# Latent tiles as raw-weight buffers from step 5 of the plain products, and product 6's loads and additions one and two steps later

## Chip, cores and metric

The kernel runs on 1 core of one Trainium2 chip. The metric is device microseconds of one execution; the time of a kernel is the median of its runs.

## What is computed

One decoder layer on 512 tokens of width 2048 in fp32, cut to what matters here:

```
h    = RMSNorm(x) * (1 + scale) + shift
proj = h @ W_in                       # 2048 x 13632
q_lat, kv_lat, k_rope, z_mla, u, v, z_sgu, g_mla, g_sgu = split(proj)
A = causal latent attention(q_lat, kv_lat, k_rope) * silu(z_mla)
B = u * (tril(W_s) v_chunk + b_s) * silu(z_sgu)
x = RMSNorm(x + gate * ((sigmoid(g_mla) * A + sigmoid(g_sgu) * B) @ W_out))
```

Every weight is used once, so the weights stream from HBM; every fp32 matmul is made of three matmuls of rounded parts (high x high, high x low, low x high).

## The kernel before

**Weights.** A `Stream` object `ws` brings each granule of weights through four stages in order. `dma_to` issues its transfer on SyncE's queue into a raw buffer; `cast_to` lets ScalarE write the high part (L139); `split_to` lets VectorE write the low part, raw minus high (L151); `get` hands both to TensorE. A raw buffer comes free when the low part is written. `look` says how many granules beyond the last split one are wanted, and no more are loaded than there are raw buffers (`held == len(self.raws)`). A buffer is either a 1024-wide tile (transfer at L98) or a pair of 512-wide tiles with a transfer for each half (L105). At first there are three: wraw0, wraw1, wraw2.

**The stretch in question.** The latents come first (16 granules of `w1`, 16 of `w2`); their last five blocks stay in PSUM banks `ps2[0..4]` and are copied to `lat8` to `lat12` (L566) by functions in `pend`, two at the first following step and one at each after. Then follow 64 steps, written out in `steps`, one granule each. The number of a granule is its step plus 32; it is the second number in the name of a tile (`wraw2_41` is step 9).

- Steps 0 to 7 ("v"): plain products into four banks and one bank z (L185 to L187).
- Steps 8 to 63: the seven products of a Strassen scheme on two sets of columns, "a" (512 wide) and "b" (384 wide), all matmuls at L701: a1 in steps 8 to 11, b1 in 12 to 15, a5 in 16 to 19, a6 in 20 to 23, b5 in 24 to 27, a2 in 28 to 31, and so on.
- Products 6, 2 and 4 need sums of weight quarters. For set a, a quarter is loaded into a chain tile raw4 to raw7 (`chain_load`, L294, SyncE's queue), and the next quarters are added to it by accumulating transfers on POOL's queue (`chain_add`, L284), which wait for the chain load to land. These granules take no raw buffer.

The normalised latents `lat0` to `lat7` lie in SBUF until they are scaled (`lat_scale`, at steps 0, 1, 1 and 3 for lat4 to lat7) and stored to DRAM (`stores`, L604, in the step after). From step 8 on, `more_raws` adds three raw buffers: w2l and the pairs (lat4, lat5) and (lat6, lat7).

**What sets the order.** The program is written in the order in which each engine runs it: step t first calls `get_step` (split of t+1, from step 10 on also the cast of t+2, transfers ahead), then the matmuls, then the small work listed by `at_step` (evacuations, squares, sums of x for the Strassen operands: `make_sums`, `split_41`), then stores. ScalarE, VectorE and SyncE each take their instructions in that order, so one that waits holds up all behind it on its engine.

After step 63 the remaining column pairs follow by the same scheme in slots of eight triples of matmuls (L1498 to L1500); their first raw weights go into wraw0 and wraw2 (`load`, L862).

Of the kernel before, what the change touches and what calls it, by code (L numbers as in the profile page):

```python
# [165 lines left out]
def trunk_layer(ctx, tc, xT, xn, c, vecs, pos, wada, w1, w2, wv, wv3, wv4, wh, wh15, wq, wqr, wk, wvv, wo, wsT, bsp, gfin, out,  # L166
# [39 lines left out]
    def nt(p, shape, dt, tag, **kw):  # L206
        uid[0] += 1
        return p.tile(shape, dt, tag=tag, name=f"{tag}_{uid[0]}", **kw)
# [10 lines left out]
    latp = Scope("lat", side=RIGHT)  # L219
    ws = Stream(nc, [(wp, f"wraw{i}") for i in range(3)], [(wp, f"w{i}") for i in range(2)])  # L220
# [58 lines left out]
    c1 = [None]  # L279
# [12 lines left out]
    def chain_load(i, c, n):  # L292
        chain[i] = t = nt(c1[0].p, [P, GW], F32, f"raw{4 + i}")
        DMA.dma_start(t[:, :n], wpair[c][0, i])  # L294
        return [t[:, :n]]

    def chain_add(i, src, n):
        return both([chain[i][:, :n]], src)
# [210 lines left out]
    def dot_to(n):  # L509
        nonlocal n_dot  # L510
        while n_dot < min(n, KC):
            ada_dot(n_dot)
            n_dot += 1
# [3 lines left out]
    def fix_to(n, between=None):  # L517

        nonlocal n_fix
        for f in rows_left:  # L520
            f()
        rows_left.clear()
        if n_fix >= min(n, KC):
            if between:
                between()
            return
        js = range(n_fix, min(n, KC))
        assert n_dot >= js[-1] + 1
        n_fix = js[-1] + 1
        cols = slice(js[0], n_fix)  # L530
        tt(shift[:, cols], dots[:, cols], vec[:, C_BADA + js[0]:C_BADA + n_fix], ALU.add)
        ts_ = []
        for j in js:
            t = nt(xq.p, [P, S], F32, "t", bufs=2)
            stt(t, xt[j], gxA[:, j:j + 1], rx, ALU.mult, ALU.mult)
            ts_.append(t)
        for j, t in zip(js, ts_):
            hh[j], hl[j] = parts_tiles(j)
            ACT.activation(hh[j], t, AF.Identity, bias=shift[:, j:j + 1])
        if between:  # L540
            between()
        for j, t in zip(js, ts_):
            stt(hl[j], t, shift[:, j:j + 1], hh[j].bitcast(F32), ALU.add, ALU.subtract)
            rows_left.append(lambda t=t, j=j: ACT.activation(xt[j], t, AF.Identity, bias=shift[:, j:j + 1]))
# [11 lines left out]
    for j in range(KC):  # L556
# [5 lines left out]
            DVE.reciprocal(out=rx[:, j * P:(j + 1) * P], in_=rx[:, j * P:(j + 1) * P])  # L562
        dot_to(DOTS[j])
        fix_to(FIXED[j])
    for m in (3, 0, 1, 2, 4):
        pend.append(lambda m=m: ACT.copy(lat[8 + m], ps2[m]))  # L566


# [33 lines left out]
    def stores():  # L602
        for dst, src in leaving:
            DMA.dma_start(dst, src)  # L604
        leaving[:], made[:] = made[:], []
# [130 lines left out]
    def run_step(t_, wH, wL):  # L736
        c, p, i = steps[t_]
        if c == "v":
            w = VW[c]
            if i == 0:  # L740
                open_banks(c, w)
                open_banks("z", S)
            for k in range(2):
                j = 2 * i + k
                sl = slice(k * w, (k + 1) * w)
                for n in range(NB):
                    tk = slice(n * P, (n + 1) * P)
                    mm3(psv[c][n], hh[j][:, tk], hl[j][:, tk], wH[:, sl], wL[:, sl], j == 0, j == KC - 1)
                sl = slice(2 * w + k * P, 2 * w + (k + 1) * P)
                mm3(psv["z"][0], wH[:, sl], wL[:, sl], hh[j], hl[j], j == 0, j == KC - 1)  # L750
        else:
            block(c, p, i, wH, wL)
        for f in early.pop(t_, ()):
            f()
# [3 lines left out]
    def get_step(t_, **kw):  # L758
        if t_ < 10:
            return get(gv[t_], **kw)  # L760
        return get(gv[t_], ahead=int(t_ < n_steps - 1), cast=gv[min(t_ + 2, n_steps - 1)], **kw)

    for t_ in range(n_steps - 4):
        if t_ == 10:
            ws.his, ws.next_hi = [(c1[0].p, "w2h", 48, 0), ws.his[1], ws.his[0]], 0
        wH, wL = get_step(t_, run=2 if t_ == 0 else 1)
        if t_ < 8:
            fix_to(FIXED[KC + t_], lambda: dot_to(DOTS[KC + t_]))
        if t_ == 8:
            ada.close()  # L770
            c1[0] = Scope("c1", side=RIGHT)
            for j in range(8):
                nt(c1[0].p, [P, S], F32R, f"e{j}")
            nt(c1[0].p, [P, GW + 48], F32R, "w2h")
            ws.more_raws([(c1[0].p, "w2l"), (latp.p, ("lat4", "lat5")), (latp.p, ("lat6", "lat7"))])
            ws.look = 9
            for i in range(4):
                chain_load(i, "a", GW)
        if t_ == 9:
            for i in range(4):  # L780
                chain_add(i, wv[1, i], GW)
        run_step(t_, wH, wL)
        stores()
# [1164 lines left out]
```

## Time and profile before

| quantity | value |
|---|---|
| median of 3 runs | 1551.08 us (1550.26 to 1553.08) |
| the profiled execution's own time | 1548.87 us |
| its span, first to last instruction | 1547.2 us |
| mean granted TensorE clock | 0.997 |
| TensorE busy | 1529.8 us (99%) |
| VectorE busy | 1194.1 us (77%) |
| ScalarE busy | 785.2 us (51%) |
| DMA engines, SyncE's queue / POOL's queue | 51.1% / 20.8% of 16 engines' span |
| HBM read / written | 310.24 / 23.94 MB |

A page of the profile describes one execution. Busy shares are averages over stages; what a change in one stage is worth is read from the timeline and the waits of that stage. A row of the timeline gives start, duration, engine, line, operation, written tile <- read tiles, form, and in brackets the idle time before it and the engine that ended it. Buffer numbers are left out of names, so `wraw` is any of wraw0 to wraw2. A DMA's own row on a queue is its issue; "us to landing" is a separate figure.

### The profile page before, as it was taken

To read this page: it belongs to the slowest core of one execution; us is meant where nothing else is said; L and a number is where in the kernel's file an instruction comes from. 1 tells how busy PE (TensorE), PEld (TensorE's weight loads), DVE (VectorE), ACT (ScalarE), POOL (GpSimd) and SP (SyncE) were. 2 spreads that over 40 slices of the span, in tenths; PEclk is the share of its full clock that TensorE was granted. 3 is DMA by queue.
4 is the path that set the end of the run, shared out by engine and by line. 5 is a ranking of instruction groups with operands and counts; after the bars stand their busy time and mean duration, and the time that the engine had idled before them with its cause. 6 is when DMAs were issued, how large, how long until landed. Compare 5 with 4: busy or idle time off the path is not lost.

```text
span 1547.2 us, 27348 instructions
## 1 busy us (share of the span) xinstructions
PE 1529.8 (99%) x10632; PEld 1425.6 (92%) x10632; DVE 1194.1 (77%) x1856; ACT 785.2 (51%) x1379; POOL 111.2 (7%) x136
## 2 busy tenths in 40 slices
PE   9999989999999999999999999999999999999997
PEld 8888978899999999999999999999888888888886
DVE  8989868878787888877787777777788888854543
ACT  4444456565645455454555646556555555632322
POOL 0000001011011111111111111121000000000000
PEclk9999999999999999999999999999999999999999
DMA  9978489788999998998888888887544344245423
GB/s 378 385 274 313 168 269 266 232 210 226 280 267 272 261 248 252 267 259 210 220 233 251 223 242 244 221 201 217 165 142 133 126 132 139 84 166 182 138 81 109
DMA packets 134580, 335.97 MB, mean 217 GB/s; under 512 B 15385, under 2 KB 39985, under 8 KB 129713
## 3 DMA queue, kind: packets, MB, share of 16 engines
q1 hardware_dynamic: 116146, 275.76, 51.1%
q0 software_dynamic: 18160, 58.20, 20.8%
q8 instruction: 83, 1.36, 0.3%
q14 instruction: 47, 0.39, 0.1%
q10 hardware_dynamic: 144, 0.26, 0.0%
HBM read 310.24 MB, written 23.94 MB: 216 GB/s over the span
## 4 chain that ended last, share of the span: by engine, by line
PE 96%; DVE 1%; DMA 1%; ACT 1%; issue 0%; DVEq 0%; POOL 0%; ACTq 0%; POOLq 0%
PE ps L1499 16%; PE ps L1498 16%; PE ps L1500 16%; PE ps L185 12%; PE ps L186 12%; PE ps L187 12%; PE ps L701 8%; PE ps L1677 1%; DMA wraw<-in_wv 1%; PE ps L1058 1%; PE ps L1641 1%; PE ps L1640 1%; PE ps L501 0%; DVE w0l L151 0%; DVE wada L176 0%
## 5 line engine op out<-in xcount | busy, mean ns | idle before, releaser
L1498 PE MATMUL ps<-h,w2h 128*128 128x256 f32 x408 | 113.8, 279 | 0.0
L1498 PE MATMUL ps<-h,w0h 128*128 128x256 f32 x408 | 113.0, 277 | 0.0
L1500 PE MATMUL ps<-h,w2l 128*128 128x256 f32 x408 | 112.7, 276 | 0.0
L1500 PE MATMUL ps<-h,w0l 128*128 128x256 f32 x408 | 112.7, 276 | 0.0
L1499 PE MATMUL ps<-h,w2h 128*128 128x256 f32 x408 | 112.7, 276 | 0.0
L1499 PE MATMUL ps<-h,w0h 128*128 128x256 f32 x408 | 112.7, 276 | 0.0
L1498 PE MATMUL ps<-h,w1h 128*128 128x256 f32 x400 | 110.9, 277 | 0.0
L1500 PE MATMUL ps<-h,w1l 128*128 128x256 f32 x400 | 110.5, 276 | 0.0
L1499 PE MATMUL ps<-h,w1h 128*128 128x256 f32 x400 | 110.5, 276 | 0.0
L139 ACT CAST w0h<-wraw 128x1024 fp32r<-128x1024 f32 (+5 forms) x71 | 61.1, 870 | 76.3 <-issue 25.3
L151 DVE TENSOR_TENSOR w0l<-wraw,w0h 128x1024 fp32r<-128x1024 f32 (+5 forms) x69 | 68.3, 997 | 39.1 <-ACT w0h L139 38.1
L173 DVE TENSOR_TENSOR w0l<-raw,w0h 128x1024 fp32r<-128x1024 f32 x56 | 68.5, 1223 | 30.0 <-ACT w0h L884 29.2
L139 ACT CAST w1h<-wraw 128x1024 fp32r<-128x1024 f32 (+5 forms) x67 | 53.9, 811 | 72.2 <-PE ps L187 24.9
L185 PE MATMUL ps<-h,w1h 128*128 128x512 f32 x218 | 86.6, 397 | 0.0
L151 DVE TENSOR_TENSOR w1l<-wraw,w1h 128x1024 fp32r<-128x1024 f32 (+5 forms) x61 | 57.8, 951 | 36.9 <-ACT w1h L139 35.7
L186 PE MATMUL ps<-h,w1h 128*128 128x512 f32 x218 | 85.0, 390 | 0.0
L187 PE MATMUL ps<-h,w1l 128*128 128x512 f32 x218 | 85.0, 390 | 0.0
L173 DVE TENSOR_TENSOR w1l<-wraw,w1h 128x1024 fp32r<-128x1024 f32 x44 | 53.9, 1224 | 36.1 <-ACT w1h L884 36.1
L173 DVE TENSOR_TENSOR w2l<-wraw,w2h 128x1024 fp32r<-128x1024 f32 x46 | 56.3, 1224 | 30.9 <-ACT w2h L884 30.9
L185 PE MATMUL ps<-h,w0h 128*128 128x512 f32 x198 | 78.0, 394 | 0.0
L187 PE MATMUL ps<-h,w0l 128*128 128x512 f32 x198 | 77.4, 391 | 0.0
L186 PE MATMUL ps<-h,w0h 128*128 128x512 f32 x198 | 77.3, 390 | 0.0
(420 smaller groups left out, 5458.5 us busy)
## 6 DMA issues: line engine op xcount, KB each, us to landing
raw<-in_wh SPq DMA_DIRECT2D x104, 512.0 KB, 6.9
wada<-in_wada SPq DMA_DIRECT2D x31, 1024.0 KB, 7.2
wraw<-in_wh POOLq DMA_DIRECT2D x55, 512.0 KB, 8.2
wraw<-in_wh SPq DMA_DIRECT2D x44, 512.0 KB, 6.2
raw<-in_wh POOLq DMA_DIRECT2D x36, 512.0 KB, 7.4
wraw<-in_wo SPq DMA_DIRECT2D x32, 512.0 KB, 3.6
half<-in_w SPq DMA_DIRECT2D x35, 256.0 KB, 5.4
wraw<-in_w SPq DMA_DIRECT2D x16, 512.0 KB, 8.6
```

Source lines behind the costliest of these rows:

```text
L139: self.nc.scalar.copy(self.hi[k][0][:, sl], src)
L151: self.nc.vector.tensor_tensor(out=lo[:, sl], in0=src, in1=hi[:, sl].bitcast(F32), op=ALU.subtract)
L173: DVE.tensor_tensor(out=out, in0=in0, in1=in1, op=op)
L185: PE.matmul(ps, ah, bh, start=start, stop=False)
L186: PE.matmul(ps, ah, bl, start=False, stop=False)
L187: PE.matmul(ps, al, bh, start=False, stop=stop)
L701: PE.matmul(psv[key][n], x_[:, tk], w_[:, sl], start=st and m == 0, stop=ch == 7 and m == 2, skip_group_check=True)
L1058: PE.matmul(ps[:, n], v[:, n], wr[:, q], start=True, stop=True)
L1498: PE.matmul(ps[:, :256], wH[:, cols[c]], xh, start=c == 0 and first, stop=False, skip_group_check=True)
L1499: PE.matmul(ps[:, :256], wH[:, cols[c]], xl, start=False, stop=False, skip_group_check=True)
L1500: PE.matmul(ps[:, :256], wL[:, cols[c]], xh, start=False, stop=c == 7, skip_group_check=True)
L1640: PE.matmul(ps, q2[:, q], krh[:, :n], start=False, stop=False)
```

## The change

- The first two entries of the order of copies L566 are swapped: lat8 (from `ps2[0]`) now comes before lat11 (from `ps2[3]`).
- The two pairs of latent tiles become raw buffers at step 5 instead of step 8, with `look` at 5; w2l still joins at step 8.
- The four chain loads of a6 are issued at step 9 instead of 8, its additions at step 11 instead of 9.

```diff
-    for m in (3, 0, 1, 2, 4):
+    for m in (0, 3, 1, 2, 4):
         pend.append(lambda m=m: ACT.copy(lat[8 + m], ps2[m]))
...
     for t_ in range(n_steps - 4):
+        if t_ == 5:
+            ws.more_raws([(latp.p, ("lat4", "lat5")), (latp.p, ("lat6", "lat7"))])
+            ws.look = 5
...
-            ws.more_raws([(c1[0].p, "w2l"), (latp.p, ("lat4", "lat5")), (latp.p, ("lat6", "lat7"))])
+            ws.more_raws([(c1[0].p, "w2l")])
             ws.look = 9
+        if t_ == 9:
             for i in range(4):
                 chain_load(i, "a", GW)
-        if t_ == 9:
+        if t_ == 11:
             for i in range(4):
                 chain_add(i, wv[1, i], GW)
```

SyncE's queue around the chain loads, before: first the load of step 8 (`wraw1_40`) and the store of lat7, then steps 9 to 12, the chain loads raw4 to raw7 (two shown of four), and steps 13 and 14.

```order
L98 DMA wraw1_40_1637<-in_wv 128x1024
L604 DMA lat_d7_111<-lat7_28_139 128x512
L98 DMA wraw2_41_1686<-in_wv 128x1024
L98 DMA wraw0_42_1735<-in_wv 128x1024
L98 DMA wraw1_43_1779<-in_wv 128x1024
L98 DMA wraw2_44_1821<-in_wv3 128x768
L294 DMA raw4_182_1836<-in_wv 128x1024
L294 DMA raw5_183_1838<-in_wv 128x1024
...
L98 DMA w2l_45_1868<-in_wv3 128x768
L105 DMA lat4_46_1870<-in_wv3 128x384
```

And now, the same place: steps 9 and 10 in latent tiles, then steps 11 to 16 (of those in latent tiles the first half is shown), the chain loads and step 17.

```order
L604 DMA lat_d7_111<-lat7_28_139 128x512
L105 DMA lat4_41_1686<-in_wv 128x512
L105 DMA lat6_42_1690<-in_wv 128x512
L98 DMA wraw2_43_1694<-in_wv 128x1024
L98 DMA wraw0_44_1743<-in_wv3 128x768
L98 DMA wraw1_45_1787<-in_wv3 128x768
L105 DMA lat4_46_1829<-in_wv3 128x384
L98 DMA w2l_47_1870<-in_wv3 128x768
L105 DMA lat6_48_1872<-in_wv 128x512
L294 DMA raw4_184_1876<-in_wv 128x1024
...
L98 DMA wraw2_49_1913<-in_wv 128x1024
```

The loads of steps 13 to 16 moved from behind the chain loads to ahead of them.

ScalarE at the end of the latents, with the copies to lat8 and lat11 between the cast of step 1's granule and the products of h:

```order
 L544 ACTIVATE x7_45_178<-t_148_1399,shift_11_88 128x512
 L139 CAST w1h_33_1432<-wraw0_33_1351 128x896
+L566 COPY lat8_29_140<-ps6_117_996 128x512
 L566 COPY lat11_32_143<-ps1_120_999 128x512
-L566 COPY lat8_29_140<-ps6_117_996 128x512
 L539 ACTIVATE h8_154_1448<-t_152_1444,shift_11_88 128x512
```

Only the two copies changed places.

SyncE's queue at the end of the 64 steps, before: the loads of steps 53, 58 and 59, two stores, then the first loads of the next stage.

```order
L98 DMA wraw1_85_2841<-in_wv3 128x768
L98 DMA wraw2_90_2928<-in_wv3 128x768
L98 DMA w2l_91_2930<-in_wv3 128x768
...
L862 DMA wraw0_258_3150<-in_wh 128x1024
L862 DMA wraw2_259_3152<-in_wh 128x1024
```

And now:

```order
L98 DMA wraw2_85_2845<-in_wv3 128x768
L98 DMA wraw0_90_2932<-in_wv3 128x768
L98 DMA wraw1_91_2934<-in_wv3 128x768
...
L866 DMA wraw0_258_3154<-in_wh 128x1024
L866 DMA wraw2_259_3156<-in_wh 128x1024
```

The rotation of the buffers has moved by one: step 58 sits in wraw0, into which the next stage's first load goes.

## The prediction

> **What bounds the kernel now.** I read the page first, then the list of waits of TensorE, then TensorE's timeline at the places of those waits, then the queues of the other engines at the same moments. The page's busy row and three rows of the waits list (engine and line, what it waited for: total us, times, longest):
>
> ```profile
> PE 1529.8 (99%) x10632; PEld 1425.6 (92%) x10632; DVE 1194.1 (77%) x1856; ACT 785.2 (51%) x1379; POOL 111.2 (7%) x136
> ...
> PE ps L701 <- DVE w1l L151: 3.7, 1, 3.7
> PE ps L701 <- DVE w0l L151: 2.5, 2, 2.1
> PE ps L185 <- ACT lat L566: 0.5, 1, 0.5
> ```
>
> TensorE sets the time, and a change that leaves its work alone can only win back waits. Nearly all of them stand at one line, L701, the plain Strassen products. I call a step by its place in `steps`: 0 to 7 are v, 8 to 11 product 1 of the first set, 12 to 15 product 1 of the second, 16 to 19 product 5 and 20 to 23 product 6 of the first. A tile's second number is the step plus 32. TensorE's timeline there (start, duration, form, idle time before and who ended it); the rows are the starts of steps 12 and 13, the three waits (in steps 14, 15 and 16), and the starts of steps 16, 17 and 18:
>
> ```profile
> 204.33 0.33 PE L701 MATMUL ps<-w1h,h 128*128 128x384 f32 x1
> 206.44 0.34 PE L701 MATMUL ps<-w0h,h 128*128 128x384 f32 x1
> ...
> 211.33 0.44 PE L701 MATMUL ps<-w0l,h 128*128 128x384 f32 x1 [2.07 <-DVE w0l L151]
> ...
> 217.44 0.69 PE L701 MATMUL ps<-w1l,h 128*128 128x384 f32 x1 [3.72 <-DVE w1l L151]
> ...
> 220.94 0.39 PE L701 MATMUL ps<-w0h,h 128*128 128x512 f32 x1
> 221.80 0.50 PE L701 MATMUL ps<-w0l,h 128*128 128x512 f32 x1 [0.46 <-DVE w0l L151]
> ...
> 224.42 0.39 PE L701 MATMUL ps<-w2h,h 128*128 128x512 f32 x1
> ...
> 227.14 0.39 PE L701 MATMUL ps<-w1h,h 128*128 128x512 f32 x1
> ```
>
> An undisturbed step of the second set takes 206.44 - 204.33 = 2.11 us, one of the first 227.14 - 224.42 = 2.72 us. Without waits step 17 would start at 204.33 + 4 x 2.11 + 2.72 = 215.49; it starts at 224.42. The loss is 8.93 us, more than the listed waits: after the long one TensorE also runs slowly. From 217.44 to 220.94 it does 11 matmuls of step 15 in 3.50 us, where a twelfth of 2.11 each makes 1.93.
>
> VectorE is named as the releaser, but it waits itself. ScalarE's casts (here the second half of step 15, and step 16) were released by transfers:
>
> ```profile
> 214.84 0.51 ACT L139 CAST w1h<-lat 128x384 fp32r<-128x384 f32 x1 [2.43 <-DMA lat<-in_wv]
> ...
> 218.76 1.14 ACT L139 CAST w0h<-wraw 128x512 fp32r<-128x512 f32 x2 [2.57 <-DMA wraw<-in_wv]
> ```
>
> SyncE's own queue says why. Loads of steps 9 to 12 leave one by one as raw buffers come free (13.86 us for four); then the four chain loads (L294), and only behind them the loads of steps 13 to 19:
>
> ```profile
> 181.86 13.86 SPq L98 DMA_DIRECT2D wraw<-in_wv  x4
> 195.77 2.73 SPq L294 DMA_DIRECT2D raw<-in_wv  x4
> ...
> 199.02 2.19 SPq L105 DMA_DIRECT2D lat<-in_wv  x4
> 202.21 1.63 SPq L98 DMA_DIRECT2D wraw<-in_wv  x2
> ...
> 208.77 0.33 SPq L98 DMA_DIRECT2D w2l<-in_wv  x1
> ```
>
> In a stretch just before, the DMA engines had room (last columns: granted clock, DMA share, GB/s); the second shows the lowered clock after the long wait:
>
> ```profile
> 185.00:190.00 5.00, 5.00 (x32) 4.74 (x31) 3.35 (x7) 2.20 (x4) 0.00 (x0) 1.00 0.29 107
> ...
> 215.00:220.00 5.00, 2.56 (x8) 2.57 (x9) 1.63 (x3) 2.43 (x6) 0.00 (x0) 0.73 1.05 231
> ```
>
> **Part 1, latent tiles as buffers from step 5.** With five raw buffers the loads of steps 9 and 10 need no buffer of the three old ones. They wait only for the stores of lat4 to lat7, the last of which leaves at 176.30 and lands 4.5 us later (the row of its landing follows the queue's):
>
> ```profile
> 176.30 0.43 SPq L604 DMA_DIRECT2D lat_d<-lat  x1
> ...
> lat_d<-lat SPq DMA_DIRECT2D x1, 256.0 KB, 4.5
> ```
>
> So they leave by 181, and every later load moves two releases forward: steps 11, 12 and 13 take the releases at 181.9 to 190.4 that served 9 to 11. Step 14 takes the buffer that the low half of step 9 gives up, step 16 that of step 10; step 15 (w2l) needs none. VectorE's two rows, and the landing of the lat load that left at 199.02:
>
> ```profile
> 194.07 1.29 DVE L151 TENSOR_TENSOR w1l<-wraw,w1h 128x512 fp32r<-128x512 f32 x2 [1.85 <-ACT w1h L139]
> ...
> 197.03 1.30 DVE L151 TENSOR_TENSOR w0l<-wraw,w0h 128x512 fp32r<-128x512 f32 x2
> ...
> lat<-in_wv SPq DMA_DIRECT2D x1, 192.0 KB, 7.4
> ```
>
> Steps 14 and 15 leave at about 195.4 to 196, step 16 at 198, all ahead of the chain loads, and no addition runs yet. Even with the 7.4 us that a load behind the chain loads took, 196 + 7.4 = 203.4 is in time for step 15 at 204.33 + 3 x 2.11 = 210.7. The waits of steps 14 to 16 go with the slow matmuls: 8.93 us. What is late next is steps 17 to 19.
>
> **Part 2, chain loads behind two more loads.** They now leave at about 198.7 instead of 195.77. The additions (L284, POOL's queue) are issued by an idle engine as soon as the chain load has landed, so their new place two steps on delays nothing by itself: the first, issued 5.7 us after its chain load, moves from 201.51 to 204.4 at most. The first and last of the four, and landings (us, last column) of the last addition and of the loads of steps 16 (left at 202.21) and 19 (208.77):
>
> ```profile
> 201.51 0.98 POOL L284 DMA_DIRECT2D raw<-in_wv  x1 [191.32 <-DVE w1l L151]
> ...
> 205.30 0.85 POOL L284 DMA_DIRECT2D raw<-in_wv  x1 [0.72 <-DMA raw<-in_wv]
> ...
> raw<-in_wv POOLq DMA_DIRECT2D x1, 512.0 KB, 15.2
> ...
> wraw<-in_wv SPq DMA_DIRECT2D x1, 512.0 KB, 16.4
> ...
> w2l<-in_wv SPq DMA_DIRECT2D x1, 512.0 KB, 15.1
> ```
>
> From 199.02 + 7.4 = 206.4 to 202.21 + 16.4 = 218.6 SyncE's queue landed 192 + 384 + 512 KB = 1.11 MB: 91 GB/s, while the additions ran (to 205.30 + 15.2 = 220.5). The two queues' shares over 150 to 250 us:
>
> ```profile
> q1 hardware_dynamic: 8137, 17.73, 51.0%
> q0 software_dynamic: 1144, 4.18, 22.1%
> ```
>
> Alone, SyncE's queue moves 17.73 MB in 51.0 us of all engines, 348 GB/s. The row of step 19 says that the last of product 5 landed at 208.77 + 15.1 = 223.9, with the queue full since step 12's load at 195.3. The same bytes stand ahead of it after the change, less the loads of steps 12 and 13 (0.79 MB, gone early): 0.79 / 348 = 2.3 us. Estimate: it lands at 221.6.
>
> A packet takes 1600 x 0.221 / 1144 = 0.31 us of an engine in the additions' queue and 1600 x 0.510 / 8137 = 0.10 in SyncE's; taking turns packet by packet leaves SyncE a quarter, 85 GB/s, near the 91 measured. By equal time for the two queues nothing would be lost here (rival B). The Trainium skill ("DMA: Bandwidth & Descriptors", Queues, rings and completion order) states just these turns, at packet granularity; it speaks against leaving the additions beside the loads of product 5, and the trace agrees with it.
>
> Between landing and use stand queues: for step 16 it took from 218.6 to 221.80, 3.2 us (its cast, then a cast of x that VectorE's next instruction needs, then its low part). Step 19 has the same, and a square on ScalarE between, whose next instruction started at 226.12:
>
> ```profile
> 225.71 0.38 ACT L633 ACTIVATE ps<-sinT 128x256 f32<-128x256 f32 x1
> ...
> 226.12 0.60 ACT L190 CAST x<-x 128x512 fp32r<-128x512 f32 x1
> ```
>
> So 3.2 + 0.4 = 3.6 us, and its second matmul runs at 225.2. Without waits it would run at 215.49 + 2 x 2.72 + 0.23 = 221.2 (0.23 = 2.72 / 12, one matmul). **Cost: 4.0 us.** A wait of step 18 lies inside that sum. Bounds: nothing, if it lands by 217.6; 6.3 us, if it lands at 223.9 as before.
>
> **Part 3, order of two copies.** v's fourth bank and the z bank wait for `ps2[0]` and `ps2[3]`, copied to lat8 and lat11, in that order on TensorE:
>
> ```profile
> 154.29 1.06 ACT L566 COPY lat<-ps 128x512 f32<-128x512 f32 x2
> ...
> 155.40 0.42 PE L185 MATMUL ps<-w0h,h 128*128 128x320 f32 x1 [0.50 <-ACT lat L566]
> ```
>
> Before, the bank needed first was copied second. Swapped, it is free one copy (0.5 us) earlier, and the z bank just in time: **0.5 us won**, at least 0.
>
> **Part 4, buffers' rotation.** The next stage's first load goes into wraw0, which step 58 now holds to the end of the products. Before, two loads left within these 11.78 us, the second in the last 0.3 us, at 323.6; the first now leaves there too. Landing took 5.1 us; the cast that needs it comes at 333.86:
>
> ```profile
> 312.12 11.78 SPq L862 DMA_DIRECT2D wraw<-in_wh  x2
> ...
> wraw<-in_wh SPq DMA_DIRECT2D x1, 512.0 KB, 5.1
> ...
> 333.86 1.13 ACT L922 CAST w0h<-wraw 128x512 fp32r<-128x512 f32 x2
> ```
>
> Two loads then, so about 330: nothing, with some 4 us of cover. The five extra half instructions on VectorE replace pairs of the same size: nothing.
>
> **Sum.** 8.9 - 4.0 + 0.5 = 5.4 us. The profiled execution took 1548.87 us (span 1547.2): 1543.5. That is 2.2 below the median of the runs, 1551.08; against the median: **1545.7 us**.
>
> **Rivals.** A is the forecast, step 19 late by 2 to 5.5 us: chance 0.5. **B, the loads of product 5 are in time:** step 12's load and the chain loads, 2.49 MB, had landed by 205.3; now steps 14 to 16 and the chain make 3.41 MB, so by 205.3 + 0.92 / 348 = 207.9. Three loads and a store remain, 1.73 MB; if SyncE's queue keeps half of the engines' time, 174 GB/s, they end at 217.8, just in time: gain 9.4, less 0.2, 1541.9. For it: idle DMA engines at 185 to 190; against it: 91 GB/s measured. 0.2. **C, the end of the loads stays at 223.9:** cost 6.3, gain 3.1, 1548.0; if the wait comes in one piece the clock drops as at 215 to 220 and costs up to 3.50 - 1.93 = 1.6 more, 1549.6. 0.2, half of it with under 3.1 us of gain. **D, slower: product 6 waits for its additions.** Step 23 starts at 225.0 + 4 x 2.72 = 235.9, so its addition must land near 233. It landed at 220.5 before, and starts at most 2.9 us later. The change is a loss if it lands after 233 + 5.4 = 238.4, and costs a microsecond for each one beyond: 1553.2 if at 240.5. For it: each chain load and addition is in series; against it: 15 us of cover. 0.05. **E, the change does not do what it says:** the latent tiles come free only at step 8; then only the copies remain, 1550.6. Against it, the store's landing by 181. 0.05.
>
> **Numbers.** A measurement of this kernel tells about 0.2%, 3.1 us, from no change. Faster: A, B and half of C, 0.8. Same: the other half of C and E, 0.15. Slower: D, 0.05. The range runs from B less 0.9 us of scatter between runs, 1541.0, to the worse half of C, 1549.0, and leaves out D, E and the tails.
>
> **What would show it.** Right: loads of steps 9 and 10 issued by 181; no wait at L701 in steps 14 and 15 and a granted clock of 1.00 from 205 to 220; chain loads at about 198.7; one or two waits in steps 18 and 19, together 2 to 5.5 us, with a cast released by a wraw transfer ahead of them; the wait at L185 near 0. Wrong: additions first issued after 205, a wait in steps 20 to 23, or a wait at L1498 after 335. The forecast fails if product 5's last load lands before 218 or after 224.

## The result and the profile after

The changed kernel took 1542.46 us (median of 4 runs, 1541.97 to 1542.77), the kernel before on the same chip 1552.08 (4 runs, 1550.26 to 1554.25): ratio 0.9937, 95% interval 0.992 to 0.9954. That is in the forecast's range and 3.2 us below its value of 1545.7; it lies nearest to rival B's 1541.9. The profiled execution took 1542.18 us, its span 1540.5; the profiled one of before 1548.87. So the two traces account for 6.7 us; the medians are further apart because that execution of before was 3.2 below its median.

The busy row of the page after, and TensorE's waits of more than 0.4 us without the one at L461, which both kernels have:

```profile
PE 1527.4 (99%) x10632; PEld 1423.8 (92%) x10632; DVE 1194.3 (78%) x1856; ACT 784.8 (51%) x1379; POOL 112.0 (7%) x136
...
PE ps L701 <- DVE w1l L151: 1.4, 1, 1.4
...
PE ps L1502 <- DVE lat L173: 0.9, 1, 0.9
PE ps L186 <- DVE h L176: 0.5, 1, 0.5
PE ps L501 <- ACT w0h L139: 0.5, 1, 0.5
```

At L701 one wait of 1.4 us is left of 6.2; the 0.5 at L185 is gone. TensorE's timeline at the places that the prediction spoke of: starts of steps 12, 16 and 19, the wait, the start of step 20.

```profile
204.03 0.33 PE L701 MATMUL ps<-w1h,h 128*128 128x384 f32 x1
...
212.38 0.39 PE L701 MATMUL ps<-w0h,h 128*128 128x512 f32 x1
...
220.58 0.39 PE L701 MATMUL ps<-w0h,h 128*128 128x512 f32 x1
222.41 0.50 PE L701 MATMUL ps<-w1l,h 128*128 128x512 f32 x1 [1.44 <-DVE w1l L151]
...
225.03 0.40 PE L701 MATMUL ps<-w2h,e 128*128 128x512 f32 x1
```

Steps 12 to 18 run without a gap; the only one is at the second matmul of step 19. Before, step 12 started at 204.33 and step 20 at 232.58. From the one to the other it takes 4 x 2.11 + 4 x 2.72 = 19.32 us without waits, so the loss of this stretch is 232.58 - 204.33 - 19.32 = 8.93 before and 225.03 - 204.03 - 19.32 = 1.68 after. I use this loss below as the measure of each kernel.

SyncE's queue after: the loads of steps 14, 15 and 16, the chain loads, the load of step 17, those of steps 18 and 19. Behind it GpSimd's queue, the first and the last of the additions, and ScalarE's cast of step 19.

```profile
194.48 0.93 SPq L105 DMA_DIRECT2D lat<-in_wv  x2
195.47 0.42 SPq L98 DMA_DIRECT2D w2l<-in_wv  x1
197.45 1.20 SPq L105 DMA_DIRECT2D lat<-in_wv  x2
198.69 2.19 SPq L294 DMA_DIRECT2D raw<-in_wv  x4
200.98 0.64 SPq L98 DMA_DIRECT2D wraw<-in_wv  x1
...
203.20 2.36 SPq L98 DMA_DIRECT2D wraw<-in_wv  x2
```

```profile
205.78 1.88 POOL L284 DMA_DIRECT2D raw<-in_wv  x2 [196.11 <-DMA raw<-in_wv]
...
209.25 0.85 POOL L284 DMA_DIRECT2D raw<-in_wv  x1 [0.18 <-issue]
```

```profile
218.96 1.14 ACT L139 CAST w0h<-wraw 128x512 fp32r<-128x512 f32 x2 [1.80 <-DMA wraw<-in_wv]
```

So step 19's load landed at 218.9 (forecast 221.6, before 223.9), and the cast that waited for it started at once. The two DMA queues after (packets, MB, share of the engines), for 205 to 210, 210 to 215 and 215 to 220; q1 is SyncE's, q0 the additions':

```profile
q1 hardware_dynamic: 801, 2.06, 103.4%
...
q0 software_dynamic: 190, 0.71, 72.4%
q1 hardware_dynamic: 207, 0.60, 33.1%
...
q0 software_dynamic: 251, 0.93, 92.8%
q1 hardware_dynamic: 251, 0.20, 15.9%
```

Until 210 SyncE's queue has the engines alone and moves 2.06 / 5 = 412 GB/s; beside the additions it moves 0.80 MB in 10 us, 80 GB/s (by the packets' sizes in the trace, 0.61 MB of it is loads up to step 19, nearly all the rest small stores). From 215 to 220 both queues have the same count of packets, 251: they take turns packet by packet, as the prediction supposed (0.31 us a packet there, 0.296 here). The additions' first packets start at 206.3 before and at 210.0 after; here are the stretches 206.2 to 206.6 and 210.0 to 210.4:

```profile
q0 software_dynamic: 12, 0.05, 78.2%
```

```profile
q0 software_dynamic: 13, 0.05, 72.8%
```

That is the key number: the contention begins 3.7 us later than before, while the loads ahead of it have lost 0.79 MB.

### The profile page after: what moved, and what is told of

Same layout as the page of the kernel before. It is cut to its first block, busy times and chain, and to the rows that moved or that the text cites. A ratio compares the mean times of both kernels' runs of the same rounds, so it can differ in the third digit from the quotient of the medians.

```text
span 1540.5 us, 27351 instructions
## 1 busy us (share of the span) xinstructions
PE 1527.4 (99%) x10632; PEld 1423.8 (92%) x10632; DVE 1194.3 (78%) x1856; ACT 784.8 (51%) x1379; POOL 112.0 (7%) x136
## 3 DMA queue, kind: packets, MB, share of 16 engines
q8 instruction: 83, 1.36, 0.3%
## 4 chain that ended last, share of the span: by engine, by line
PE 94%; DMA 3%; ACT 1%; DVE 1%; issue 1%; SPq 0%; DVEq 0%; ACTq 0%; POOL 0%; POOLq 0%
PE ps L1502 15%; PE ps L1503 15%; PE ps L1504 15%; PE ps L186 12%; PE ps L185 12%; PE ps L187 12%; PE ps L701 7%; PE ps L1681 1%; DMA wraw<-in_wv 1%; PE ps L1062 1%; DMA wraw<-in_w 1%; PE ps L1645 1%; PE ps L1644 1%; DMA half<-in_pos 0%; DMA raw<-in_wv 0%
## 5 line engine op out<-in xcount | busy, mean ns | idle before, releaser
L1502 PE MATMUL ps<-h,w0h 128*128 128x256 f32 x408 | 113.1, 277 | 0.9 <-DVE lat L173 0.9
L1502 PE MATMUL ps<-h,w2h 128*128 128x256 f32 x408 | 113.8, 279 | 0.0
L1502 PE MATMUL ps<-h,w1h 128*128 128x256 f32 x400 | 110.9, 277 | 0.0
L151 DVE TENSOR_TENSOR w0l<-wraw,w0h 128x1024 fp32r<-128x1024 f32 (+5 forms) x61 | 63.7, 1047 | 38.6 <-ACT w0h L139 38.1
L185 PE MATMUL ps<-h,w1h 128*128 128x512 f32 x218 | 86.6, 397 | 0.0
L185 PE MATMUL ps<-h,w0h 128*128 128x512 f32 x198 | 78.1, 394 | 0.0
L1502 PEld LDWEIGHTS ps<-h,w0h 128*128 128x128 f32 x408 | 76.6, 188 | 1.0 <-issue 1.0
```

What stands on the lines that cost most here:

```text
L151: self.nc.vector.tensor_tensor(out=lo[:, sl], in0=src, in1=hi[:, sl].bitcast(F32), op=ALU.subtract)
L185: PE.matmul(ps, ah, bh, start=start, stop=False)
L1502: PE.matmul(ps[:, :256], wH[:, cols[c]], xh, start=c == 0 and first, stop=False, skip_group_check=True)
```

## Experiments

Theory T came from this: **what of SyncE's queue is still to move when the additions' first packets run goes at about 80 GB/s instead of 400, so small differences ahead of that moment become microseconds at step 19.** The rivals are named in each expectation. Losses are from step 12 to step 20, as above, in the one profiled execution.

| kernel | median us (runs) | ratio to before, 95% | step 12, step 20 start | loss |
|---|---|---|---|---|
| before | 1552.08 (4) | | 204.33, 232.58 | 8.93 |
| changed | 1542.46 (4) | 0.992 to 0.9954 | 204.03, 225.03 | 1.68 |
| e1_copies | 1551.77 (11) | 0.9991 to 1.0011 | 204.14, 233.86 | 10.40 |
| e2_buffers | 1545.80 (5) | 0.9949 to 0.9972 | 203.92, 228.92 | 5.68 |
| e3_move | 1546.79 (6) | 0.9956 to 0.998 | 204.52, 228.60 | 4.76 |
| e4_add9 | 1541.92 (6) | 0.9928 to 0.9953 | 204.11, 229.23 | 5.80 |
| e5_chain10 | 1540.41 (6) | 0.9924 to 0.9951 | 203.65, 223.08 | 0.11 |
| e6_chain11 | 1543.81 (6) | 0.9944 to 0.9968 | 204.12, 223.39 | -0.05 |
| e7_halves | 1543.61 (5) | 0.9939 to 0.9963 | 204.07, 223.34 | -0.05 |
| e8_noadd | 1543.25 (5) | 0.9938 to 0.9962 | 204.27, 226.06 | 2.47 |
| e9_after | 1544.03 (6) | 0.9937 to 0.9966 | 204.18, 228.69 | 5.19 |
| e10_nocopies | 1545.03 (5) | 0.9946 to 0.997 | 204.49, 225.41 | 1.60 |
| e11_dose | 1546.56 (5) | 0.9955 to 0.9981 | 204.35, 229.77 | 6.10 |
| e12_spread | 1540.11 (5) | 0.9916 to 0.9939 | 204.37, 223.63 | -0.06 |

The kernel before, run beside them, had medians of 1551.31 (e1 to e4), 1551.58 (e5 to e8) and 1551.38 us (e9 to e12).

### e1: the copies alone

```
 # kernel before
-    for m in (3, 0, 1, 2, 4):
+    for m in (0, 3, 1, 2, 4):
```

> Kernel before with only the two copies of v swapped. Theory T (the three parts act apart, and the copies win the wait of 0.50 us at 155.40): 0.3 to 0.5 us less than before, 1551.6, which one comparison can hardly tell from nothing; the row of that wait is gone and step 12 of the products starts 0.3 to 0.5 us earlier. Rival R (the copies set when the first loads find room, and so carry part of the gain): 1.5 us or more, 1550.5 or less.

The wait at 155 is gone from the list, and in the trace step 12 starts 0.19 us earlier, less than T's 0.3 to 0.5; but the time is that of before within 0.1%, some 1.5 us either way, too coarse to tell 0.5 us from nothing. Rival R is out: the copies carry no part of the gain that a comparison can see.

### e2: early buffers without the move of the chain

```
 # changed kernel
+        if t_ == 8:
-        if t_ == 9:
             for i in range(4):
                 chain_load(i, "a", GW)
-        if t_ == 11:
+        if t_ == 9:
             for i in range(4):
                 chain_add(i, wv[1, i], GW)
```

> Changed kernel with the chain loads and the additions put back to where they stood (steps 8 and 9); the early latent buffers and the copies stay. Theory T (SyncE's queue moves at 350 to 410 GB/s until the first packet of an addition and at about 90 GB/s beside them; in the changed kernel those packets start at 209.5 and step 19 lands at 218.9): the additions start about 4 us earlier here, the load of step 19 lands at 221 to 223, the wait in step 19 is 3.5 to 6 us instead of 1.4, and the time is 2 to 4 us above the changed kernel, 5.5 to 7.5 us below before. Rival S (early buffers alone carry all the gain): the same as the changed kernel within 1 us, 9 us below before.

GpSimd's first addition, then TensorE's waits in steps 17 and 18:

```profile
201.02 0.98 POOL L284 DMA_DIRECT2D raw<-in_wv  x1 [191.29 <-DVE w1l L151]
```

```profile
216.10 0.50 PE L701 MATMUL ps<-w1l,h 128*128 128x512 f32 x1 [0.69 <-DVE w1l L151]
221.22 0.51 PE L701 MATMUL ps<-w1h,h 128*128 128x512 f32 x1 [2.29 <-ACT w1h L139]
```

The additions start 4.8 us earlier than in the changed kernel and steps 17 and 18 are late. The three old waits are gone, as T and S both had it; the loss of 5.68 lies in product 5 alone. 1545.80 is 5.5 below before and 3.3 above the changed kernel's 1542.46: T, not S. (Some later executions of the changed kernel took as long, see e9; all five of e2 did.) The lateness came in step 18 rather than 19.

### e3: the move of the chain without early buffers

```
 # kernel before
+        if t_ == 9:
             for i in range(4):
                 chain_load(i, "a", GW)
-        if t_ == 9:
+        if t_ == 11:
```

> Kernel before with only the chain loads and additions moved to steps 9 and 11; no early buffers, copies as before. Theory T (the chain loads' place ahead of steps 13 to 16 made the three waits; the early buffers only bring the queue forward): the waits of steps 14 to 16 shrink to under 1 us in sum, the loads of steps 11 and 12 now stand in the same stretch, so step 19 lands 2 to 5 us later than in the changed kernel and waits 3.5 to 6 us: 3 to 6 us below before. Rival M (moving the chain loads does it all): 8 us or more below before. Rival B (the early buffers are what does it): within 2 us of before, with waits in steps 14 to 16 that remain.

TensorE's two waits of product 5, then GpSimd's first additions:

```profile
221.71 0.51 PE L701 MATMUL ps<-w0h,h 128*128 128x512 f32 x1 [0.31 <-ACT w0h L139]
224.48 0.50 PE L701 MATMUL ps<-w1l,h 128*128 128x512 f32 x1 [2.26 <-DVE w1l L151]
```

```profile
207.92 1.88 POOL L284 DMA_DIRECT2D raw<-in_wv  x2 [196.71 <-DVE w0l L151]
```

Without a single early buffer the waits of steps 14 to 16 are gone too. The additions leave even later than in the changed kernel, but the loads of steps 11 and 12 now stand in the same stretch, and step 19 is late. 4.5 us below before: T's time and landing lie within its bounds, its wait does not (2.6 us in sum instead of 3.5 to 6; slow matmuls behind it, with a granted clock of 0.66 from 225 to 230, make up most of the rest of the loss of 4.76). M and B are out. Each half of the change alone removes the three old waits; together they also shorten the new one.

### e4: additions two steps earlier in the program

```
 # changed kernel
-        if t_ == 11:
+        if t_ == 9:
             for i in range(4):
                 chain_add(i, wv[1, i], GW)
```

> Changed kernel with the additions issued two steps earlier in the program (step 9, right behind the chain loads); all else the same. Theory T (an addition leaves when its chain load has landed, GpSimd has nothing else to do): first addition at 205.5 to 206, the wait of step 19 at 1.2 to 1.6 us, time within 0.5 us of the changed kernel. Rival P (the two steps in the program hold the additions back and so keep the stretch free for product 5): first addition 2 us or more earlier, step 19 waits 3 us or more, 2 us slower than the changed kernel.

GpSimd's first additions in the trace:

```profile
205.62 1.88 POOL L284 DMA_DIRECT2D raw<-in_wv  x2 [194.38 <-DVE w1l L151]
```

205.62 against 205.78 and 1541.92 against 1542.46: rival P is out, the two steps in the program hold nothing back. The prediction said so. What T missed is in the same run: five executions took 1541.10 to 1542.66 us, and the profiled one 1546.29, with a loss of 5.80 although its additions start within 0.2 us of the changed kernel's. From 205 to 210 its queue moved 1.72 MB, not 2.06.

### e5 and e6: chain loads later still

```
 # changed kernel; e5: chain loads at 10; e6: chain loads at 11, additions at 12
-        if t_ == 9:
+        if t_ == 10:
             for i in range(4):
                 chain_load(i, "a", GW)
```

> Changed kernel with the four chain loads one step later (step 10, behind the load of step 17); additions as in the changed kernel. Theory T (in the changed kernel about 0.75 MB of SyncE's queue up to step 19 is still to move when the additions' packets start at 209.5, and moves at 80 GB/s; alone it would take 1.9 us): the additions start 1.5 to 3 us later, steps 18 and 19 land by 213, TensorE's wait of 1.4 us in step 19 is gone: 1 to 2 us below the changed kernel, 10 to 11.5 below before; product 6 in time. Rival D (product 6 then waits for its additions): a wait in steps 20 to 23, time equal to the changed kernel or above.

e5's queues from 210 to 215, and the cast of step 19:

```profile
q0 software_dynamic: 167, 0.62, 65.6%
q1 hardware_dynamic: 191, 0.72, 39.5%
```

```profile
217.01 1.14 ACT L139 CAST w0h<-wraw 128x512 fp32r<-128x512 f32 x2 [2.12 <-DMA wraw<-in_wv]
```

No wait at L701 and a loss of 0.11: the time is as T had it, five of six executions at 1540.24 to 1540.61 (one at 1546.57). Its way there was not: the additions start at 205.98, only 0.2 us later, since the chain loads now land faster; step 19 lands at 217.0, not by 213. Bytes do not explain the 1.9 us by which the landing moved: SyncE's queue moved 0.72 MB from 210 to 215 instead of 0.60, but from 195 to 215 it moved 5.07 instead of 5.13. What differs is how evenly the 16 DMA engines were along (last point of the next section).

> Changed kernel with the chain loads two steps later (step 11, behind the load of step 18) and the additions issued at step 12. Theory T: product 5 has SyncE's queue alone; additions leave at about 210, move alone at about 190 GB/s and land at 217 to 226, each some 2 us ahead of the cast that needs it: as e5 within 1 us. Rival D (product 6 late): waits of 1 to 4 us in steps 20 to 23, 1 to 4 us slower than the kernel with the loads at step 10.

In e6 product 5 ends in time, and all four casts of steps 20 to 23 wait for additions, 0.8 to 2.0 us each (steps 21 and 23 shown); TensorE waits in product 5 of the second set, behind them:

```profile
221.57 1.14 ACT L139 CAST w1h<-raw 128x512 fp32r<-128x512 f32 x2 [1.96 <-DMA raw<-in_wv]
...
227.69 1.14 ACT L139 CAST w2h<-raw 128x512 fp32r<-128x512 f32 x2 [1.54 <-DMA raw<-in_wv]
```

```profile
236.12 0.44 PE L701 MATMUL ps<-w1h,h 128*128 128x384 f32 x1 [1.17 <-ACT ps L642]
...
241.75 0.44 PE L701 MATMUL ps<-w0l,h 128*128 128x384 f32 x1 [1.52 <-DVE w0l L151]
```

1543.81, 3.4 above e5. This is the prediction's rival D, product 6 late, in another guise: steps 20 to 23 themselves do not wait, but ScalarE and VectorE fall behind and steps 24 and later pay. T had missed it; from e5 to e6 the chain loads moved behind one more load, and the additions one step on.

### e7: the additions in halves

```
 # changed kernel
-                chain_add(i, wv[1, i], GW)
+                both([chain[i][:, :S], chain[i][:, S:]], wv[1, i])
```

> Changed kernel with each of the four additions issued as two halves of 512 columns, so their packets are half as long; bytes and places the same. Theory T (the queues take turns packet by packet, so SyncE's share beside the additions is set by the length of their packets): SyncE moves clearly more than the 0.20 to 0.24 MB per us-quintet of 212 to 220 in the changed kernel (50 to 100 GB/s there, 80 to 150 here), step 19 lands 2 to 4 us earlier, its wait of 1.4 us goes, 1 to 1.6 us below the changed kernel. Rival V (the share goes by bytes or by time, whatever the packets): the wait stays at 1 us or more, time as the changed kernel within 0.5 us.

The queues from 215 to 220, the cast of step 19, and a wait of TensorE far behind:

```profile
q0 software_dynamic: 433, 0.79, 85.7%
q1 hardware_dynamic: 438, 0.32, 26.5%
```

```profile
216.14 1.14 ACT L139 CAST w0h<-wraw 128x512 fp32r<-128x512 f32 x2 [0.57 <-DMA wraw<-in_wv]
```

```profile
1072.74 0.50 PE L185 MATMUL ps<-h,w1h 128*128 128x512 f32 x1 [0.57 <-ACT w1h L139]
```

With packets half as long the counts are again equal, 433 and 438, and SyncE's queue moves 0.32 MB instead of 0.20 (from 212 to 220, 78 GB/s instead of 66, just under T's 80 to 150). Step 19 lands 2.8 us earlier, and its wait and the whole loss are gone: the turns by packet are shown, V is out. The next stage starts at 327.75 instead of 329.51. The total did not follow: 1543.61, above the changed kernel's 1542.46, because this trace waits 1.9 us between 1000 and 1085 for weights, where the changed kernel waits 0.1. Whether the edit brings that about or these five executions happened on it is open.

### e8: no additions for product 6 of the first set

```
 # kernel before
-        if t_ == 9:
-            for i in range(4):
-                chain_add(i, wv[1, i], GW)
```

> Kernel before without the four additions to the chain for product 6 of the first set, so product 6 of the first set is worked out from the loaded halves alone. All loads and their order as before. Theory T (the additions' packets beside them make the loads late, not the four chain loads ahead of them): steps 14 to 19 land at 348 to 410 GB/s, all by 212, the waits of steps 14 to 16 shrink to under 1 us in sum with no slowed clock behind: 8 to 10 us below before. Rival C (the chain loads' 2 MB ahead in the queue, as the prediction named the cause): the waits of steps 14 and 15 stay at 2 us and more, 1 to 5 us below before.

What is left of the waits at L701 in steps 13 and 14:

```profile
206.89 0.44 PE L701 MATMUL ps<-w0h,h 128*128 128x384 f32 x1 [0.34 <-ACT w0h L139]
207.48 0.44 PE L701 MATMUL ps<-w1l,h 128*128 128x384 f32 x1 [0.15 <-DVE w1l L151]
...
211.02 0.44 PE L701 MATMUL ps<-w0l,h 128*128 128x384 f32 x1 [1.17 <-DVE w0l L151]
```

8.3 us below before, with every chain load in its old place. The long waits of steps 15 and 16 and the slow matmuls are gone, and of the 8.93 lost 2.47 stay: with the chain loads in their old place, the additions made 6.5 us of the loss. The two causes do not simply add: e3, which moves chain loads and additions together behind the loads of steps 13 to 16, has no wait left there at all. T gave under 1 us of waits and it was 1.7, so rival C has a share, but the small one.

### e9 to e12: the changed kernel again, copies, dose, spread

> The changed kernel again, unedited, so that the three kernels below stand beside it on the same chip. All theories: 1541.5 to 1543 us, 8.5 to 10 below before; an execution some 4 us above the others can occur if less than the usual 2 MB moves in 205 to 210.

```
 # e10: changed kernel
-    for m in (0, 3, 1, 2, 4):
+    for m in (3, 0, 1, 2, 4):
```

> Changed kernel with the two copies of v back in their old order. Theory K (the copies win the 0.5 us of the wait at 155.40, as the prediction put it): 0.3 to 0.6 us above the changed kernel in the medians, and the wait at about 155 is back. Rival N (the wait only moves: a start 0.3 us earlier is given back at the wait of step 19, which is set by a transfer): the wait at 155 is back, the time is the same within 0.2 us, and the wait of step 19 is shorter by what the other is longer.

The changed kernel gave 1541.10, 1541.48 and 1542.24, and 1545.82, 1545.93 and 1547.82 us. With the four runs of the result, seven executions lie at 1541.1 to 1542.8 and three some 4 us later; e9's median is above the 1541.5 to 1543 that was expected. The profiled one was of the later kind, although 1.94 MB, nearly the usual 2, moved from 205 to 210:

```profile
224.46 0.51 PE L701 MATMUL ps<-w1l,h 128*128 128x512 f32 x1 [2.26 <-DVE w1l L151]
```

Its additions start at 206.04, its loss is 5.19. e10's trace shows the wait at v back, and step 19's wait hardly shorter (1.36):

```profile
155.57 0.41 PE L185 MATMUL ps<-w0h,h 128*128 128x320 f32 x1 [0.51 <-ACT lat L566]
```

Its medians cannot be set against e9's: with 1542.40 to 1547.16 beside 1541.10 to 1547.82, the two kinds hide 0.5 us. K and N stay open on time; the trace, in which the step-19 wait did not shorten by 0.5, speaks against N.

```
 # e11: changed kernel; dose_d is a scratch that nothing reads
                 chain_load(i, "a", GW)
+            DMA.dma_start(dose_d, hh[0].bitcast(F32))
```

> Changed kernel with one extra store of 256 KB in SyncE's queue behind the chain loads and ahead of the load of step 17 (it writes a tile of h to a scratch that nothing reads; the output is the same). Theory T (what is still to move when the additions' packets start goes at 50 to 80 GB/s until they end): the 0.26 MB cost 3 to 5 us at the landing of step 19, which comes at 221.5 to 224; waits of steps 18 and 19 sum to 4 to 6 us; 3 to 5 us above the changed kernel. Rival L (the queue's bytes count at its rate alone, 348 GB/s, as the prediction's 0.79 MB = 2.3 us did): 0.75 us later, 0.5 to 1 us above the changed kernel.

TensorE's wait in step 18 (L702 is the old L701, a line further down), and the cast of step 19:

```profile
222.00 0.52 PE L702 MATMUL ps<-w1h,h 128*128 128x512 f32 x1 [3.66 <-ACT w1h L139]
```

```profile
223.71 1.14 ACT L139 CAST w0h<-wraw 128x512 fp32r<-128x512 f32 x2 [0.36 <-DMA wraw<-in_wv]
```

All five executions take 1545.96 to 1547.12, 2.5 us above e9's median and about 5 above its lower kind, which e11 never shows. 256 KB that cost 0.75 us by L's rate put step 19's cast at 223.71, 4.8 us behind the changed kernel's first trace and 2.7 behind e9's (221.02). T's landing fits; its waits sum to 3.9 us, just under the 4 to 6. Against e9 the intervals overlap, and the additions started 0.7 us earlier here (205.09) than in the first trace, so the time alone does not rule out L.

```
 # e12: changed kernel
-        if t_ == 9:
-            for i in range(4):
+        if t_ in (10, 11):
+            for i in range(2 * (t_ - 10), 2 * (t_ - 9)):
                 chain_load(i, "a", GW)
-        if t_ == 11:
-            for i in range(4):
+        if t_ in (11, 12):
+            for i in range(2 * (t_ - 11), 2 * (t_ - 10)):
                 chain_add(i, wv[1, i], GW)
```

> Changed kernel with the chain loads and additions in two pairs: loads at steps 10 and 11, additions at 11 and 12 (the second pair of loads stands behind step 18's). Theory T: only step 19's load meets additions, and only two of them; it lands by 216, no wait in product 5; the later pair of additions lands at 222 to 227, in time for steps 22 and 23: 1 to 2 us below the changed kernel, as the kernel with all four at step 10, without executions 4 us above the rest. Rival D (the later pair is late for product 6): a wait in steps 22 to 25, time at or above the changed kernel.

SyncE's two pairs of chain loads, GpSimd's third addition, the cast of step 19:

```profile
201.69 0.90 SPq L294 DMA_DIRECT2D raw<-in_wv  x2
...
204.22 1.13 SPq L294 DMA_DIRECT2D raw<-in_wv  x2
```

```profile
211.26 0.84 POOL L284 DMA_DIRECT2D raw<-in_wv  x1 [2.40 <-DMA raw<-in_wv]
```

```profile
217.25 1.14 ACT L139 CAST w0h<-wraw 128x512 fp32r<-128x512 f32 x2 [2.27 <-DMA wraw<-in_wv]
```

1540.11 (1539.77 to 1541.28), the lowest median of the table, 0.3 us below e5's, which is no difference: no loss, no execution among five that ends 4 us later, no late product 6. Up to the cast of step 19 the additions had moved 0.82 MB here, less than two of them, and 1.44 MB in the changed kernel; whether that or the engines' even pace (last point of the next section) did it is not separated. Step 19 lands at 217.2 all the same, 1.2 us after T's bound and within the 217.6 that the prediction gave as the bound of no cost.

## Why the prediction was right, and where its size was off

- **What bounds the kernel: half right.** The waits and the loss of 8.93 were read rightly. The cause, "the four chain loads, and only behind them the loads of steps 13 to 19", is the smaller part: without additions (e8) 2.5 us of loss stay. The additions' packets beside those loads make 6.5, and they come when the chain loads have landed, so moving the chain loads (e3) takes away both. The prediction named the additions only for product 5.
- **Part 1, 8.9 us: right.** Loads of steps 9 and 10 left by 181 and steps 14 to 16 had no wait, with a granted clock of 1.00 from 205 to 220 (the third column from the right; then DMA share and GB/s):

```profile
205.00:210.00 5.00, 5.00 (x31) 5.00 (x30) 3.39 (x7) 4.36 (x10) 3.47 (x4) 1.00 1.03 412
...
215.00:220.00 5.00, 5.00 (x24) 4.14 (x23) 2.65 (x5) 3.06 (x7) 0.00 (x0) 1.00 1.09 225
```

But e3 removes the same waits without part 1.
- **Part 2, cost 4.0 us: right mechanism, mis-sized.** Chain loads at 198.69 (198.7 forecast), one wait in step 19, a cast released by a wraw transfer, 3.5 us from landing to matmul (3.6), 80 GB/s beside the additions (85): all as written. The step that failed is "the first, issued 5.7 us after its chain load, moves from 201.51 to 204.4 at most". It moved to 205.78, past the 205 that the prediction had set as a sign of error: the chain loads now share the queue with steps 14 to 16 and took longer:

```profile
raw<-in_wv SPq DMA_DIRECT2D x4, 512.0 KB, 7.8
```

The first addition's extra 1.4 us, at 400 GB/s for the loads, is 0.56 MB that no longer had to go at 80 GB/s; as an estimate that is worth up to 5.6 us, while the landing came 2.7 us earlier than forecast, so the sum does not close. The other half of the failed step is "0.79 / 348 = 2.3 us": bytes ahead of the contention were priced at the queue's own rate (412 GB/s where it ran alone, not 348); e11 speaks for a higher price, 2.7 to 4.8 us for 0.26 MB. Landing 218.9 instead of 221.6; cost 1.68 in this trace, not 4.0. In e9's trace it is 5.19. The forecast's 4.0 falls between the two kinds, and it was luck that the four runs of the result were all of the better one.
- **Part 3, 0.5 us: the wait went, the gain stays unmeasured** (e1, e10).
- **Part 4, nothing: right.** The next stage's first load left at 316 and its cast had no wait for it. A wait of 0.9 us does stand at L1502 (L1498 before) at 356, the sign that the prediction had called wrong. The copies alone (e1), which leave the rotation untouched, show it too, at 1.4; so it isn't the rotation. It gives 0.9 back of the 7.6 us won by step 20, which leaves the 6.7 between the two traces.
- **Rivals.** B's time came out nearly right for a wrong reason: SyncE's queue did not keep half of the engines' time beside the additions but 33% and then 16%. C, as a sum, is what e11 and the later kind of execution look like. D was rightly improbable here and begins two loads later (e6).
- **The later kind of execution, and what the theory missed.** Neither the start of the additions (issued within 0.4 us in the first four traces below) nor the bytes still to move order the landings. What goes with a late landing is 16 DMA engines that are far apart. A load counts as landed when all 16 shares have; the trace records each. Landings are in us, first to last share; the last column counts the loads' packets of 4096 bytes not yet moved when the additions' first packet started:

| trace | last chain load landed before the additions' packets | step 19's load, first / 8th / last share | packets left |
|---|---|---|---|
| changed, first trace | 206.76 to 208.96 | 212.74 / 214.36 / 218.86 | 165 |
| e9, later kind | 206.86 to 209.39 | 212.26 / 214.02 / 220.93 | 141 |
| e4, later kind | 207.07 to 209.48 | 214.15 / 215.10 / 223.08 | 190 |
| e5 | 209.07 to 209.45 | 215.68 / 216.27 / 216.91 | 185 |
| e12 | 210.35 to 210.73 | 216.19 / 216.55 / 217.15 | 168 |

e9 had the fewest packets left and its 8th share landed earliest of all, and yet the whole load landed 2 us after the first trace's: its last three shares, 1.4 to 2.1 us behind the 8th at the chain load, were 3.6 to 6.9 us behind it at step 19's. In e5 and e12 SyncE's queue had run dry for 0.9 us (at 200.7 and at 201.3) and the engines were within 0.4 us of each other afterwards; in the other three it never ran dry from 195 to 206. That the pause evened them out is argued, not shown: e6 had one too (at 201.1), and its engines were 1.9 us apart again at 208. Why engines fall behind stays open, and so does e5's one execution at 1546.57, of which there is no trace.

## What to carry to other kernels

Where two DMA queues meet, look for the moment when the second one's packets begin, and ask what of the first queue is still to move then: it goes at the contended rate, everything ahead of that moment at the full one, so a few hundred KB can cost microseconds, more than their own transfer time (e11). Look at the last of the DMA engines to land, not at the sum of the bytes. Where executions of one kernel fall into two groups, give it slack: spreading the second queue's work (e12) won it, and pushing it back as a whole went too far one load beyond e5 (e6).

## What the runs showed of the hardware

- An addition of GpSimd's queue moves its first packet long after its issue: 4.2 us in the changed kernel (205.78 to 210.0), 4.4 in e12 (206.91 to 211.3), but 2.2 in e8 (225.22 to 227.4), where SyncE's queue was idle until 226 and took 52% of the engines after. The Trainium skill ("DMA: Bandwidth & Descriptors", Latency and other measured facts) gives about 1 us to the first byte on this path; these traces show two to four times that, and least in the quietest stretch.
- Packets of the two queues come out in equal numbers, 251 to 251 and 433 to 438, whatever their length. The Trainium skill ("DMA: Bandwidth & Descriptors", Queues, rings and completion order) says turns at packet granularity; the traces agree.
- Beside the additions a queue of short packets suffers most: from 215 to 220 SyncE's packets held 0.20 MB / 251 = 0.8 KB each, and got 40 GB/s. Most were not of loads but of small stores that stand behind them: 113 packets of 1024 bytes and 94 of 256, against 15 of 4096.
- The 16 DMA engines do not keep step: the shares of one load landed over 6 to 9 us beside the additions in the changed kernel and e4, and over 1.0 to 1.2 us in e5 and e12.
